# Walking the moving columns and the output of a float32r matmul in runs of 16

## The chip, the cores and the metric

The kernel runs on one core of one Trainium2 chip, as one launch. The metric is the device time of that core in microseconds. The inputs lie in HBM, laid out with channels on partitions, and the output is written back to HBM in the same way.

## The reference

Two layers of a diffusion backbone over 256 latent tokens and 256 context tokens, each of 2048 channels, in float32. Layer 0 mixes tokens by pooling over windows of 2, 4, 8 and 16; layer 1 by neighbourhood attention that also reads the context. Each mixer is followed by a gated feed-forward of inner width 5504 with a width-3 convolution along the tokens. Shift, scale and gate of every sub-layer come from a modulation of two conditioning vectors. What matters here is the feed-forward:

```python
def conv_ffn(u, w_gate, w_up, conv_w, conv_b, w_down):
    T = u.shape[1]
    gp = jnp.pad(u @ w_gate, ((0, 0), (1, 1), (0, 0)))
    gte = gp[:, :T] * conv_w[0] + gp[:, 1:T + 1] * conv_w[1] + gp[:, 2:] * conv_w[2] + conv_b
    return (jax.nn.silu(gte) * (u @ w_up)) @ w_down

    ...
    h = h + ml[:, 5] * conv_ffn(modulate(rms_norm(h, norm2_g[i]), ml[:, 3], ml[:, 4]), ...)
    if not last:
        hc = hc + mc[5] * conv_ffn(modulate(rms_norm(hc, norm2_g[i]), mc[3], mc[4]), ...)
```

In layer 0 it runs for both streams, latent and context; in layer 1, the last, for the latent one alone.

## The kernel before

Activations are kept transposed: a tile has 128 channels on its partitions and tokens along the free dimension. There are 16 such tiles of channels (KT), and the inner width of the feed-forward makes 43 tiles (NF). One PSUM bank is 128 x 512 float32, and every output of the matmuls in question is one bank or half of one.

To keep float32 accuracy on TensorE's faster float32r format, every operand is split into a high part, rounded to float32r, and a low part, the rest. A weight tile is loaded from HBM on SP's queue, ACT casts its high part and DVE (or POOL) subtracts to get the low part (`split`, L145 and L147). A product is then three terms: high times high, high weight times low activation, low weight times high activation.

- **Layer 0, gate and up** (`gu0`, L638 to L640). For each of the 35 tiles from 8 on, one gate and one up bank are filled. The 512 columns are the 256 latent and the 256 context tokens. For each of the 16 channel tiles `A[k]` three matmuls follow one another: high weight with the high columns (L638), high weight with the low columns (L639), low weight with the high columns (L640). The first eight tiles are made earlier, during the mixer (`partial`, L551 to L553).
- **Layer 0, down** (`down0`, L664 to L666). The 43 tiles are taken in chunks of four (three in the last). For each chunk and each of the 16 output tiles, the same three matmuls are made for each tile of the chunk, over `acts`, which are pairs of high and low 512-column tiles.
- **Layer 1, gate and up** (`gu1`, L773 and L776). There are only 256 columns. The high and the low columns of a channel tile lie side by side in `B[k]`, so one matmul of 512 columns (L773) does two of the three terms, each into its half of the bank; a matmul of 256 columns (L776) adds the low weight's term into the second half. Eight of the first kind, eight of the second, then again eight and eight.
- **Layer 1, down** (`down1`, L820 and L824; L816 to L818 for the last chunk) has the same form as gate and up.
- **Attention** lies between the layers: values (L883 to L885), keys (L948 to L950), queries (L967 and L971), output projection (L1092 and L1134).

All of these matmuls write to whole, unbroken pieces of a bank, and read unbroken runs of columns. L967 alone reads its 512 columns as two runs of 256, which lie 512 columns apart in `A[k]`.

The order of the instructions on each engine is set when the program is built, by a scheduler that goes over the whole kernel. Banks are handed out from pools: four for gate and up, three or four for down. During layer 0's feed-forward DVE also computes the modulation of layer 1 (`pump`, L245 and L247), with a small matmul per piece that sums over partition groups (L171). After each down projection ACT scales the bank (L676, L833), and POOL adds it to the residual stream `hl` and `hc` (L677, L835).

Of the kernel before, what the change touches and what calls it, by code (L numbers as in the profile page):

```python
# [17 lines left out]
P = 128  # L18
D = 2048
KT = D // P  # L20
T = 256
# [38 lines left out]
def kernel(ctx: ExitStack, tc: tile.TileContext, xT, cxT, wmod, wg, wu, wd, wp,  # L60
                         wq, wv, wo, vec, cc, rope, inv, strips, out):
    nc = tc.nc
# [8 lines left out]
    def bank(tag, name):  # L71

        if tag == "d" and nbank[0] is not None:
            nbank[0] += 1
            if nbank[0] % 4 == 0:
                tag = "m"
        return pp.tile([P, 512], F32, tag=tag, bufs={"gu": 4, "d": 3, "m": 1}[tag], name=name)

    def flat(a):
        return a.rearrange("p s t -> p (s t)")  # L80


    vt = main.tile([P, NVEC], F32, name="vt")
# [39 lines left out]
    def load(src, cols, name):  # L123

        ts = []
        for j in range(0, cols, 1024):
            n = min(1024, cols - j)
            t = stage(f"{name}_{j}")
            nc.sync.dma_start(t[:, :n], src(j, j + n))
            ts.append((t, n))  # L130
        return ts

    def split(ts, name, share=0):

        parts = []
        for j, (t, n) in enumerate(ts):
            turn[0] += 1
            pools = [whp] * 3 + extra
            pool = pools[turn[0] % len(pools)]
            hi = pool.tile([P, 1024], F32R, tag="wh", name=f"{name}h{j}")  # L140
            lo = pool.tile([P, 1024], F32R, tag="wl", name=f"{name}l{j}")
            with ExitStack() as behind:
                for ins in hold:
                    behind.enter_context(tc.issue_after(ins))
                nc.scalar.copy(hi[:, :n], t[:, :n])  # L145
                eng = nc.gpsimd if share and turn[0] % share == 0 else nc.vector
                eng.tensor_tensor(lo[:, :n], t[:, :n], hi[:, :n].bitcast(F32), op=ALU.subtract)  # L147
            parts.append((hi, lo))
        return parts

    def ld(src, name, share=0):
        return split(load(lambda a, b: src[:, a:b], 2048, name), name, share)
# [114 lines left out]
    def M(l, which, k, s):  # L267
        return modT[l, which * 4 + k // 4][:, k % 4, s : s + 1]
# [60 lines left out]
    with ExitStack() as ph0:  # L329
# [6 lines left out]
        for j in range(1, 4):  # L336
            nc.vector.tensor_copy(quad[:, j], quad[:, 0])
        quad = flat(quad)

        def h_of(s):  # L340
            return hc if s else hl
# [46 lines left out]
        acts = {}  # L388
# [238 lines left out]
        def gu0(f):  # L627
            res = []
            for nm, wsrc in (("g", wg), ("u", wu)):
                parts = ld(wsrc[0, f], f"w{nm}0_{f}")  # L630
                if f > NS + 3:
                    next(pump, None)
                ps = bank("gu", f"{nm}0_{f}")
                for k in range(KT):
                    hi, lo = parts[k // 8]
                    c = P * (k % 8)
                    xh, xl = flat(A[k][:, 0]), flat(A[k][:, 1])
                    nc.tensor.matmul(ps, hi[:, c : c + P], xh, start=(k == 0), stop=False)  # L638
                    nc.tensor.matmul(ps, hi[:, c : c + P], xl, start=False, stop=False)  # L639
                    nc.tensor.matmul(ps, lo[:, c : c + P], xh, start=False, stop=(k == KT - 1))  # L640
                    if k == 7 and f > NS + 3:
                        next(pump, None)
                res.append(ps)
            return res
# [3 lines left out]
        def down0(c, fs, acts, after=None):  # L648
            n = len(fs)
            last = c == len(chunks) - 1  # L650
            for mg in range(4):
                parts = split(load(lambda a, b: wd[0, mg, :, fs[0] + a // 512 : fs[0] + b // 512, :], 512 * n, f"wd0_{c}_{mg}"),
                              f"wd0_{c}_{mg}")
                if c > 1:
                    next(pump, None)
                for m in range(4):
                    if m == 2 and c > 1:
                        next(pump, None)
                    ps = bank("d", f"d0_{c}_{mg}_{m}")
                    for i in range(n):  # L660
                        hi, lo = parts[i // 2]
                        o = 512 * (i % 2) + P * m
                        xh, xl = acts[i]
                        nc.tensor.matmul(ps, hi[:, o : o + P], xh, start=(i == 0), stop=False)  # L664
                        nc.tensor.matmul(ps, hi[:, o : o + P], xl, start=False, stop=False)  # L665
                        nc.tensor.matmul(ps, lo[:, o : o + P], xh, start=False, stop=(i == n - 1))  # L666
                    k = 4 * mg + m
                    if last:
                        for s in both:
                            nc.vector.scalar_tensor_tensor(h_of(s)[:, k, :], ps[:, T * s : T * s + T], M(0, 5, k, s),  # L670
                                                           h_of(s)[:, k, :], op0=ALU.mult, op1=ALU.add)
                        n3.add(h_of, k)
                    else:
                        y = f0.tile([P, 2, T], F32, tag="t2", name=f"dy{c}_{k}")
                        for s in both:
                            nc.scalar.activation(y[:, s], ps[:, T * s : T * s + T], AF.Copy, scale=M(0, 5, k, s))  # L676
                            nc.gpsimd.tensor_tensor(h_of(s)[:, k, :], h_of(s)[:, k, :], y[:, s], op=ALU.add)  # L677
                if after is not None:
                    after()
# [3 lines left out]
        acts[NC], sg = gate0(NC, *r6)  # L683
        normalise(0, 3, h_of, both, rstd, f0, range(14, KT))
        res = gu0(NS)
        rest = [e for e in range(NS) if e not in acts]

# [33 lines left out]
    with ExitStack() as ph2:  # L721
# [11 lines left out]
        B = {}  # L733

        def norm_b(ks):
            for k in ks:
                a = ap0.tile([P, 2, 2, T], F32R, tag=f"A{k}", name=f"B{k}")[:, 0]
                y = f1.tile([P, 512], F32, tag="t2", name=f"nrmB{k}")[:, 0:T]
                nc.vector.scalar_tensor_tensor(y, hl[:, k, :], M(1, 4, k, 0), rstd[:, 0:T], op0=ALU.mult, op1=ALU.mult)
                nc.scalar.activation(a[:, 0], y, AF.Identity, bias=M(1, 3, k, 0))  # L740
                if k % 2:
                    z = f1.tile([P, 512], F32, tag="t2", name=f"nrmBz{k}")[:, 0:T]
                    nc.scalar.activation(z, y, AF.Identity, bias=M(1, 3, k, 0))
                    nc.gpsimd.tensor_tensor(a[:, 1], z, a[:, 0].bitcast(F32), op=ALU.subtract)
                else:
                    ins = nc.vector.scalar_tensor_tensor(a[:, 1], y, M(1, 3, k, 0), a[:, 0].bitcast(F32),
                                                         op0=ALU.add, op1=ALU.subtract)
                B[k] = a
                if k == 9:
                    hold[:] = [ins.ins]  # L750

        def gu1(f):
            res = []
            pre = None
            if f == 0:
                pre = [load(lambda a, b: w[1, f][:, a:b], 2048, f"w{nm}1_{f}") for nm, w in (("g", wg), ("u", wu))]
                for q, ts in enumerate(pre):
                    first = split(ts[:1], f"w{q}1_{f}_0", 4)
                    hold[:] = [tail]
                    pre[q] = first + split(ts[1:], f"w{q}1_{f}_1", 4)  # L760
                    hold.clear()
                norm_b(range(KT))
            elif f == 2:
                hold.clear()
            for q, (nm, wsrc) in enumerate((("g", wg), ("u", wu))):
                parts = pre[q] if pre else ld(wsrc[1, f], f"w{nm}1_{f}", 2 if f % 4 > 1 else 0)
                ps = bank("gu", f"{nm}1_{f}")

                for j in range(2):
                    hi, lo = parts[j]  # L770
                    for k in range(8 * j, 8 * j + 8):
                        c = P * (k % 8)
                        nc.tensor.matmul(ps, hi[:, c : c + P], flat(B[k]), start=(k == 0), stop=False)  # L773
                    for k in range(8 * j, 8 * j + 8):
                        c = P * (k % 8)
                        nc.tensor.matmul(ps[:, T:], lo[:, c : c + P], B[k][:, 0], start=False, stop=(k == KT - 1))  # L776
                res.append(ps)
            return res

# [60 lines left out]
        for c, fs in enumerate(chunks):  # L840
            acts = []
# [16 lines left out]
        for j, (a, b) in enumerate(((0, 4), (4, 6), (6, 8), (8, 12), (12, 16))):  # L858
            v = hl[:, a:b, :]
# [379 lines left out]
```

## Time and profile before

| | us |
|---|---|
| median of 2 runs (3069.73 to 3072.13) | 3070.93 |
| the profiled execution | 3070.34 |
| its span, from the first to the last instruction | 3068.5 |
| PE busy in the span | 3007.0 |
| DVE busy | 1939.4 |
| ACT busy | 1372.9 |
| POOL busy | 826.4 |

PE is the engine that runs the matmuls, PEld its weight loads; every matmul of the trace has a weight load of its own. DVE, ACT and POOL are the vector, scalar and general engines, SP the queue from which the loads are issued. A matmul's record goes from its start to its end, and the next one begins before it ends; so the records overlap, and the rate of the stream is read from the distance of the starts. Rows of one line give the instruction count after an x, then the shortest, the median and the longest duration in ns, and the first and the last start in us. Rows of the chain of waits give the start, the length and what ran, merged where one line follows itself. PEclk is the TensorE clock that was granted.

### The profile page before, as it was taken

What the parts mean: (1) busy time and instruction counts of PE and PEld (TensorE: products, weight loads), DVE (VectorE), ACT (ScalarE), POOL (GpSimd) and SP (SyncE); (2) the same over time, 40 slices, a digit from 0 to 9 for tenths busy, and PEclk for the clock granted to TensorE, in tenths of its full rate; (3) what the DMA queues carried; (4) which work ended last, traced back from release to release, by engine and by line L of the source; (5) the groups of instructions that cost most, each with busy time, mean ns of one, the idle gap of its engine ahead of it and who ended that gap; (6) DMA issues with size and microseconds to landing.
All of it is one profiled execution on the core that took longest, in us unless ns stands there. A gap on an engine that the chain in (4) does not pass through costs nothing.

```text
span 3068.5 us, 40828 instructions
## 1 busy us (share of the span) xinstructions
PE 3007.0 (98%) x15082; PEld 2414.2 (79%) x15082; DVE 1939.4 (63%) x2748; ACT 1372.9 (45%) x2219; POOL 826.4 (27%) x823
## 2 busy tenths in 40 slices
PE   6999999999999999999999999999999999999998
PEld 2565658888888888888887888878888888888887
DVE  4445774285674857658485666474767666666666
ACT  3333454423333242433334444343545666666665
POOL 2011213303022130311302000000002566566665
PEclk9999999999999999999999999999999999999999
DMA  9878663284755747466482333333355556565553
GB/s 382 334 271 305 215 233 103 90 253 141 223 178 180 226 148 250 148 203 202 161 253 83 113 108 104 106 112 106 106 159 184 183 180 201 189 188 180 185 192 117
DMA packets 177927, 559.70 MB, mean 182 GB/s; under 512 B 17600, under 2 KB 22208, under 8 KB 177728
## 3 DMA queue, kind: packets, MB, share of 16 engines
q1 hardware_dynamic: 177728, 557.10, 55.6%
q8 instruction: 119, 1.95, 0.3%
q14 instruction: 80, 0.66, 0.1%
HBM read 554.93 MB, written 2.10 MB: 182 GB/s over the span
## 4 chain that ended last, share of the span: by engine, by line
PE 94%; DVE 2%; POOL 1%; DMA 1%; ACT 1%; issue 1%; SPq 0%; DVEq 0%; ACTq 0%; POOLq 0%
PE g L773 5%; PE u L773 5%; PE d L664 5%; PE d L666 5%; PE d L665 5%; PE d L820 4%; PE g L638 4%; PE g L640 4%; PE g L639 4%; PE u L639 4%; PE u L638 4%; PE u L640 4%; PE mod L199 3%; PE u L776 3%; PE g L776 3%; PE d L824 2%
## 5 line engine op out<-in xcount | busy, mean ns | idle before, releaser
L677 POOL TENSOR_TENSOR hl<-hl,dy 128x256 f32<-128x256 f32 x160 | 146.7, 917 | 943.3 <-ACT dy L676 943.1
L835 POOL TENSOR_TENSOR hl<-hl,dy 128x256 f32<-128x256 f32 x320 | 332.2, 1074 | 188.2 <-ACT dy L833 186.0
L247 DVE SCALAR_TENSOR_TENSOR macc<-wm,sc,macc 128x512 f32<-128x512 f32 (+1 forms) x360 | 328.9, 946 | 70.8 <-DMA wm<-wmod 69.8
L676 ACT ACTIVATE dy<-d,modT 128x256 f32<-128x256 f32 x320 | 133.1, 469 | 187.1 <-PE d L666 172.4
L199 PE MATMUL mod<-wm,sc 128*32 128x512 f32 x768 | 131.1, 617 | 23.3 <-DMA wm<-wmod 23.3
L677 POOL TENSOR_TENSOR hc<-hc,dy 128x256 f32<-128x256 f32 x160 | 129.0, 806 | 0.0
L833 ACT ACTIVATE dy<-d,modT 128x512 f32<-128x512 f32 x160 | 104.5, 684 | 43.0 <-PE d L824 41.5
L147 DVE TENSOR_TENSOR wd_2l<-wd,wd_2h 128x1024 fp32r<-128x1024 f32 (+1 forms) x44 | 54.6, 1247 | 108.8 <-ACT wd_2h L145 107.6
L922 POOL TENSOR_TENSOR rk<-rk,rp 128x256 f32<-128x256 f32 x16 | 13.2, 826 | 365.5 <-DVE rk L921 309.7
L147 DVE TENSOR_TENSOR wd_3l<-wd,wd_3h 128x1024 fp32r<-128x1024 f32 (+1 forms) x44 | 52.0, 1203 | 76.8 <-ACT wd_3h L145 75.5
L147 DVE TENSOR_TENSOR wd_1l<-wd,wd_1h 128x1024 fp32r<-128x1024 f32 (+1 forms) x44 | 53.7, 1225 | 56.4 <-ACT wd_1h L145 56.4
L472 POOL TENSOR_TENSOR pf<-ws,inv 128x256 f32<-128x256 f32 x32 | 27.7, 885 | 220.6 <-PE mod L199 105.0
L199 PEld LDWEIGHTS mod<-wm,sc 128*32 128x32 f32 x768 | 23.7, 110 | 77.4 <-issue 61.5
L145 ACT CAST wd_1h<-wd 128x1024 fp32r<-128x1024 f32 (+1 forms) x44 | 45.3, 1031 | 78.3 <-PE u L639 53.5
L147 DVE TENSOR_TENSOR wd_0l<-wd,wd_0h 128x1024 fp32r<-128x1024 f32 (+1 forms) x44 | 54.7, 1249 | 36.9 <-ACT wd_0h L145 36.9
L1011 ACT ACTIVATE sb<-sb,nm 128x512 f32<-128x512 f32 x64 | 46.1, 722 | 64.3 <-DVE nm L1007 63.1
L799 DVE TENSOR_TENSOR actb<-sgb,actb 128x256 fp32r<-128x256 f32 x43 | 52.8, 1228 | 26.2 <-ACT actb L798 26.2
L145 ACT CAST wd_0h<-wd 128x1024 fp32r<-128x1024 f32 (+1 forms) x44 | 45.2, 1031 | 53.6 <-PE u L773 29.1
L664 PE MATMUL d<-act,wd_2h 128*128 128x512 f32 x172 | 67.2, 391 | 0.0
L666 PE MATMUL d<-act,wd_2l 128*128 128x512 f32 x172 | 67.0, 390 | 0.0
L665 PE MATMUL d<-act,wd_2h 128*128 128x512 f32 x172 | 67.0, 390 | 0.0
L666 PE MATMUL d<-act,wd_3l 128*128 128x512 f32 x172 | 67.0, 390 | 0.0
(1752 smaller groups left out, 9278.0 us busy)
## 6 DMA issues: line engine op xcount, KB each, us to landing
wm<-wmod SPq DMA_DIRECT2D x384, 512.0 KB, 6.1
wd<-wd SPq DMA_DIRECT2D x168, 512.0 KB, 4.4
wg<-wg SPq DMA_DIRECT2D x156, 512.0 KB, 4.7
wu<-wu SPq DMA_DIRECT2D x156, 512.0 KB, 4.5
wv<-wv SPq DMA_DIRECT2D x32, 512.0 KB, 4.0
wk<-wq SPq DMA_DIRECT2D x32, 512.0 KB, 4.1
wq<-wq SPq DMA_DIRECT2D x32, 512.0 KB, 3.6
wo<-wo SPq DMA_DIRECT2D x32, 512.0 KB, 3.9
```

The lines of the kernel that those rows point to most:

```text
L147: eng.tensor_tensor(lo[:, :n], t[:, :n], hi[:, :n].bitcast(F32), op=ALU.subtract)
L199: nc.tensor.matmul(ps[32 * j : 32 * j + 32, :], sc[:, 4 * g + j, :], ts[j // 2][0][:, 512 * (j % 2) : 512 * (j % 2) + 512], start=(g == 0) ...
L247: nc.vector.scalar_tensor_tensor(acc[s], v, sc2[:, k, s : s + 1], acc[s], op0=ALU.mult, op1=ALU.add)
L638: nc.tensor.matmul(ps, hi[:, c : c + P], xh, start=(k == 0), stop=False)
L639: nc.tensor.matmul(ps, hi[:, c : c + P], xl, start=False, stop=False)
L640: nc.tensor.matmul(ps, lo[:, c : c + P], xh, start=False, stop=(k == KT - 1))
L664: nc.tensor.matmul(ps, hi[:, o : o + P], xh, start=(i == 0), stop=False)
L665: nc.tensor.matmul(ps, hi[:, o : o + P], xl, start=False, stop=False)
L666: nc.tensor.matmul(ps, lo[:, o : o + P], xh, start=False, stop=(i == n - 1))
L677: nc.gpsimd.tensor_tensor(h_of(s)[:, k, :], h_of(s)[:, k, :], y[:, s], op=ALU.add)
L773: nc.tensor.matmul(ps, hi[:, c : c + P], flat(B[k]), start=(k == 0), stop=False)
L835: nc.gpsimd.tensor_tensor(hl[:, k, :], hl[:, k, :], y[:, q], op=ALU.add)
```

## The change

A helper gives another view of the same columns: the free dimension is seen as a x n x 16, and walked with the n in front. For n = 4 and 512 columns, the walk takes columns 0 to 15, then 64 to 79, 128 to 143 and so on to 463, then it starts again at 16, at 32 and at 48. For n = 2 the runs of 16 lie 32 columns apart and there are two rounds. The moving operand and the output of a matmul are walked in the same order, so each column's product lands where it did before.

It is used in the three places named above: layer 0's gate (n = 4) and up (n = 2), layer 0's down (n = 4), and layer 1's gate and up (n = 4, both the 512- and the 256-column matmuls). Layer 1's down, attention, the mixer and the first eight tiles of layer 0 are as before.

```diff
+    def turns(v, n=4):
+
+        return v.rearrange("p (a b e) -> p b a e", b=n, e=16)
...
                     xh, xl = flat(A[k][:, 0]), flat(A[k][:, 1])
-                    nc.tensor.matmul(ps, hi[:, c : c + P], xh, start=(k == 0), stop=False)
-                    nc.tensor.matmul(ps, hi[:, c : c + P], xl, start=False, stop=False)
-                    nc.tensor.matmul(ps, lo[:, c : c + P], xh, start=False, stop=(k == KT - 1))
+                    n = 4 if nm == "g" else 2
+                    xh, xl, po = turns(xh, n), turns(xl, n), turns(ps, n)
+                    nc.tensor.matmul(po, hi[:, c : c + P], xh, start=(k == 0), stop=False)
+                    nc.tensor.matmul(po, hi[:, c : c + P], xl, start=False, stop=False)
+                    nc.tensor.matmul(po, lo[:, c : c + P], xh, start=False, stop=(k == KT - 1))
...
-                        xh, xl = acts[i]
-                        nc.tensor.matmul(ps, hi[:, o : o + P], xh, start=(i == 0), stop=False)
-                        nc.tensor.matmul(ps, hi[:, o : o + P], xl, start=False, stop=False)
-                        nc.tensor.matmul(ps, lo[:, o : o + P], xh, start=False, stop=(i == n - 1))
+                        xh, xl = map(turns, acts[i])
+                        po = turns(ps)
+                        nc.tensor.matmul(po, hi[:, o : o + P], xh, start=(i == 0), stop=False)
+                        nc.tensor.matmul(po, hi[:, o : o + P], xl, start=False, stop=False)
+                        nc.tensor.matmul(po, lo[:, o : o + P], xh, start=False, stop=(i == n - 1))
...
-                        nc.tensor.matmul(ps, hi[:, c : c + P], flat(B[k]), start=(k == 0), stop=False)
+                        nc.tensor.matmul(turns(ps), hi[:, c : c + P], turns(flat(B[k])), start=(k == 0), stop=False)
...
-                        nc.tensor.matmul(ps[:, T:], lo[:, c : c + P], B[k][:, 0], start=False, stop=(k == KT - 1))
+                        nc.tensor.matmul(turns(ps[:, T:]), lo[:, c : c + P], turns(B[k][:, 0]), start=False, stop=(k == KT - 1))
```

## The prediction

> **What bounds the kernel now.** I read the head of the page first, then the busy time in stretches of the span, then the rows of the changed lines and the chain of waits for the spacing of the matmuls.
>
> ```profile
> span 3068.5 us, 40828 instructions
> PE 3007.0 (98%) x15082; PEld 2414.2 (79%) x15082; DVE 1939.4 (63%) x2748; ACT 1372.9 (45%) x2219; POOL 826.4 (27%) x823
> PEclk9999999999999999999999999999999999999999
> PE 94%; DVE 2%; POOL 1%; DMA 1%; ACT 1%; issue 1%; SPq 0%; DVEq 0%; ACTq 0%; POOLq 0%
> ```
>
> PE is busy for 98% of the span, and 94% of the chain that ended last is PE. Its clock is not held back. The stretches say the same for the two places that the change touches:
>
> ```profile
> core 0: us, PE busy (x) PEld busy (x) DVE busy (x) ACT busy (x) POOL busy (x), PEclk, DMA share, GB/s
> 500.00:1650.00 1150.00, 1150.00 (x5095) 953.33 (x5094) 732.01 (x902) 407.49 (x619) 246.59 (x296) 1.00 0.59 183
> 2330.00:3020.00 690.00, 690.00 (x3937) 606.05 (x3936) 465.71 (x475) 424.33 (x623) 416.11 (x341) 1.00 0.58 187
> ```
>
> The first stretch is the feed-forward of layer 0 (gate, up, down), the second that of layer 1. In both, PE has no idle time, and the next busiest engine, DVE, has 64% (732 of 1150) and 67% (466 of 690). So every nanosecond by which a matmul's place in the stream grows or shrinks goes into the end of the kernel whole.
>
> A busy PE is not its rate, since the records overlap (a matmul is in flight for some 390 ns while the next has begun). The rate is the distance from start to start:
>
> ```profile
> L638 PE MATMUL g<-A,wg_10h x16: 389/390/390, 525.8 to 536.0; 128*128 128x512 f32 x16
> 2363.88 0.23 PE u L773
> 2364.11 0.95 PE u L776 x8
> 2365.06 1.84 PE g L773 x8
> 2366.90 0.95 PE g L776 x8
> L816 PE MATMUL d<-actb,wd_0h x12: 283/284/284, 3036.3 to 3040.3; 128*128 128x256 f32 x12
> ...
> L816 PE MATMUL d<-actb,wd_2h x12: 283/283/284, 3044.9 to 3048.9; 128*128 128x256 f32 x12
> ```
>
> The first row is one gate tile of layer 0: L638, L639 and L640 take turns, so from the first to the last of 16 lie 45 matmuls in 10.2 us, 226.7 ns each, for 512 columns. The next rows are pieces of the chain (start, length, what): in layer 1 eight 512-column matmuls take 1.84 us (230 ns each) and eight 256-column ones 0.95 us (119 ns). The two L816 rows stand 72 matmuls of 256 columns apart (two groups of 4 x 3 x 3): 8.6 us, 119.4 ns each. So one column costs (226.7 - 119.4) / 256 = 0.419 ns, 512 columns 214.5 ns, and some 12 ns of every matmul do not depend on the columns.
>
> **The change, part by part.** Only access patterns change. Each engine's instructions stand in the order of before, SP's and POOL's DMA and work included, with the same tiles and counts; nothing is moved past a queue, nothing is added to ACT, DVE or POOL. What PSUM holds at the end of a group is at the same addresses, so its readers see no difference. Nineteen matmuls of the down projection lose a wait of PE on PE: it is an in-order engine that idles 0 in that stretch, so I cost this at nothing.
>
> How many matmuls are walked otherwise:
>
> ```profile
> 0.00:3069.00 3069.00, 437.08 (x1120) 210.41 (x1120) 0.99 0.56 182
> 0.00:3069.00 3069.00, 268.13 (x688) 129.22 (x688) 0.99 0.56 182
> 0.00:3069.00 3069.00, 349.43 (x1376) 249.70 (x1376) 0.99 0.56 182
> 0.00:3069.00 3069.00, 192.25 (x1376) 187.29 (x1376) 0.99 0.56 182
> ```
>
> These are the rows of L638, L664, L773 and L776 alone over the whole span (counts in brackets). L638 to L640 are 3 x 1120 = 3360, half with a step of 64 (gate) and half with 32 (up); L664 to L666 are 3 x 688 = 2064; L773 is 1376: together 6800 of 512 columns. L776 is 1376 of 256. A walk of 512 columns in runs of 16 has 32 runs and 31 jumps, whichever step; one of 256 has 15. Sum: 6800 x 31 + 1376 x 15 = 231,440 jumps, each made by the reading side (SBUF) and by the writing side (PSUM) at once. All lie on PE, without cover.
>
> What a jump costs is not in the trace for the writing side: every output of before is one unbroken run. For the reading side there is one near row. L967 (attention's queries) reads 512 columns as two runs of 256 that lie 512 apart, and writes one run:
>
> ```profile
> 1890.32 1.81 PE q L967 x8
> ```
>
> That is 226 ns each, no more than the unbroken L638, with half a step of the last digit, 0.6 ns, as the room for one jump. So a jump in reading is free or costs at most about 0.6 ns. The far end is to treat each run of 16 as a matmul of its own; the nearest row is the sum of the layer-1 modulation:
>
> ```profile
> 1007.37 0.13 PE modt_12s L171 x2
> 1007.82 0.13 PE modt_13s L171 x2
> ```
>
> 0.13 us for two of 16 columns, 65 ns each, 32 of them 2.1 us in place of 0.227: some 12.7 ms in all. Nothing in the program splits the instruction, so I use it for no case but as the end that is excluded.
>
> The other end is a gain. It can be no more than what stands beside the columns: 5424 x (226.7 - 214.5) = 66 us, 1376 x (230 - 214.5) = 21 us, 1376 x (119 - 107.3) = 16 us, 103 us together, if the walk removed all of it. Those 12 ns are the same at 512 and at 256 columns, which speaks for a price of the instruction or its weight load, and not for one of the walk.
>
> For a jump I take one column's time, 0.419 ns: it is the smallest step by which a stream of one column after the other can slip, it lies within the 0.6 ns that L967 leaves, and the writing side must add to what stands in PSUM at full rate, column after column, with no slack that any row shows. Sum: 231,440 x 0.419 ns = 97 us. On the profiled execution's own 3070.3 us that is 3167 us; the median of the runs shown, 3070.9, is 0.6 us above it, which changes nothing. Per line I expect 240 ns in place of 226.7 for the 512-column matmuls of layer 0, 243 for 230 at L773, and 125 for 119 at L776.
>
> [...]
>
> **What else could lie behind it.** The end of the kernel is not PE's:
>
> ```profile
> 3021.76 27.24 POOL hl L835 x28
> ```
>
> The last adds of layer 1 on POOL follow the down projection, which is not changed in layer 1. If PE is slower in gate and up, POOL comes to this stretch with the same work or less behind it; I add nothing.
>
> **Rivals.** (1) A jump is free on both sides: 3070 us. For it: the L967 row, the same engine, type and column count. Against it: one jump is not 31, and the row has none in the output. [...]
>
> (2) Faster. What stands beside the columns is not quite fixed: L773 is spaced 230 ns where L638 has 226.7 for the same columns, type and tile size, and the weight loads behind them differ too:
>
> ```profile
> L664 PEld LDWEIGHTS d<-act,wd_0h x172: 187/188/188, 460.3 to 1648.3; 128*128 128x128 f32 x172
> L816 PEld LDWEIGHTS d<-actb,wd_0h x12: 192/192/193, 3036.2 to 3040.1; 128*128 128x128 f32 x12
> ```
>
> 187 ns in the even stream, 192 in the stream of short matmuls. That looks like two reads, of the weights and of the moving columns, that hinder each other by their phase. If the excess comes from addresses that fall together, a walk in steps of 128 or 256 bytes can take them apart. The price is up to 103 us, so down to 2967 us; it decides (2% is 61 us) once 60% of the excess goes. Against it: A, B and the activations lie in different tiles and columns, and all 512-column rows of layer 0 still have the same 226.7 ns.
>
> (3) A jump costs more: two columns' time, for example where reading and writing both slip, 194 us, 3264 us; at three, 3361 us. A price that is some half of a run's own time (8 columns, 3.4 ns) would give 3070 + 776 = 3846 us. For it speaks only that nothing bounds the writing side.
>
> (4) The step matters, not the jump: with 32 free and 64 at one column's time, the 1680 up matmuls drop out, 1680 x 31 x 0.419 ns = 22 us, and the time is 3145 us. I count it with the forecast, since it is on the same side.
>
> **How the numbers follow.** A slower kernel through jumps has 0.52: 0.28 at about one column's time (with the fourth rival), 0.10 at about two, 0.14 at more. No change has 0.23, faster by the second rival 0.25, spread from 2967 to 3009 us. The forecast is the likeliest price of the likeliest side, 3167 us, its own range 3135 to 3200. The range for 8 in 10 reaches over both signs: from 2975 (which leaves out 0.05 of the gain) to 3270 (two columns' time; it leaves out 0.14). Slower by over 2%, which is about what a measurement of this kernel can tell from no change, is over 3132 us, faster is under 3010 us: 0.52 slower, 0.23 within, 0.25 faster.
>
> **What would show it.** In the profile after, the start-to-start distance of the changed lines is the whole test: some 240 ns in a layer-0 gate tile (45 matmuls in 10.8 us in place of 10.2), eight L773 in 1.94 us and eight of the 256-column line in 1.0 us, with the unchanged L820 spaced as before, and the stretches outside the two feed-forwards equally long. Gate and up of layer 0 side by side tell whether the step counts. The first rival shows as 226.7 ns, the second as less than that with a shorter weight load, the third as well over 240. The prediction is wrong if these distances stay while the time moves, or if an unchanged line's distance changes.

## The result and the profile after

The changed kernel takes 3146.78 us (median of 2 runs, 3145.79 to 3147.78) against 3070.93 us; the ratio is 1.0247, 95% interval 1.0203 to 1.0291. That is 76 us more, where 97 us were forecast. The profiled execution took 3145.79 us, with a span of 3144.0.

The head of the page and, in the second fence, the busy time of the two feed-forward stretches (the second one moved to later times):

```profile
span 3144.0 us, 40828 instructions
PE 3085.2 (98%) x15082; PEld 2419.9 (77%) x15082; DVE 1934.7 (62%) x2748; ACT 1373.4 (44%) x2219; POOL 825.1 (26%) x823
```

```profile
core 0: us, PE busy (x) PEld busy (x) DVE busy (x) ACT busy (x) POOL busy (x), PEclk, DMA share, GB/s
500.00:1650.00 1150.00, 1150.00 (x4826) 909.39 (x4825) 704.01 (x873) 380.30 (x568) 218.97 (x265) 1.00 0.57 175
2400.00:3100.00 700.00, 700.00 (x3957) 606.45 (x3956) 464.75 (x476) 426.95 (x627) 419.31 (x343) 1.00 0.58 185
```

The same instructions, the same clock (PEclk 1.00), no idle time (PE busy 1150.00 of 1150.00 us), but in the same 1150 us PE gets through 4826 matmuls instead of 5095. Nothing waits more; each matmul takes longer. The rows of one gate and one up tile of layer 0 (step 64 and step 32), and pieces of the chain of waits from layer 1 (start, length, what):

```profile
L645 PE MATMUL g<-A,wg_10h x16: 395/402/411, 531.4 to 542.1; 128*128 128x512 f32 x16
L645 PE MATMUL u<-A,wu_10h x16: 398/403/407, 542.9 to 553.6; 128*128 128x512 f32 x16
```

```profile
2490.28 0.92 PE d L827 x4
...
2521.22 1.90 PE u L780 x8
2523.13 0.94 PE u L783 x8
2524.07 1.89 PE g L780 x8
```

From the first to the last of the 16 lie 45 matmuls: 10.7 us, 238 ns each, in both tiles. In layer 1, L780 (before the change L773) takes 1.90 us for eight where it took 1.84, and L783 (L776) 0.94 where it took 0.95. L827 (L820), which is not changed, stays at 0.92 for four; before it was 0.93.

A row's times end at a tenth of a us, which leaves such a distance open by 2 ns. For the sum and for the experiments I therefore average the distance from each matmul's start to the next one's over all records of the line in the trace (1680 gate, 1680 up, 2064 down, 1376 long and 1376 short ones of layer 1), without the few distances over 1.25 times the median:

| mean distance, ns | before | after | difference | over all records, us |
|---|---|---|---|---|
| layer 0 gate (runs of 16, step 64) | 227.0 | 239.2 | +12.2 | +20.5 |
| layer 0 up (runs of 16, step 32) | 226.7 | 240.0 | +13.3 | +22.3 |
| layer 0 down (step 64) | 226.7 | 239.5 | +12.8 | +26.1 |
| layer 1 gate and up, 512 columns | 230.3 | 237.8 | +7.5 | +9.2 |
| layer 1 gate and up, 256 columns | 119.1 | 117.8 | -1.3 | -1.8 |

The last column sums every distance, the long ones too: 76.3 us, which is the whole of the 76.

Layer 1's long matmuls also lose less because they had lost something before. By place in their group of eight, the distances of before are 233, 236, 228, 232, 231 and three times 227 ns (medians): behind the short matmuls it takes five long ones to reach the pace of layer 0. That is why their mean was 230.3 and not 226.7. After the change the eight are 237, 232, 236, 239, 242, 240, 238 and 241 ns.

### The profile page after: what moved, and what is told of

Same layout as the page of the kernel before. It is cut to its first block, busy times and chain, and to the rows that moved or that the text cites. A ratio compares the mean times of both kernels' runs of the same rounds, so it can differ in the third digit from the quotient of the medians.

```text
span 3144.0 us, 40828 instructions
## 1 busy us (share of the span) xinstructions
PE 3085.2 (98%) x15082; PEld 2419.9 (77%) x15082; DVE 1934.7 (62%) x2748; ACT 1373.4 (44%) x2219; POOL 825.1 (26%) x823
## 4 chain that ended last, share of the span: by engine, by line
PE 95%; DVE 1%; POOL 1%; DMA 1%; ACT 1%; issue 1%; SPq 0%; DVEq 0%; ACTq 0%; POOLq 0%
PE g L780 5%; PE d L671 5%; PE d L673 5%; PE d L672 5%; PE u L780 5%; PE d L827 4%; PE g L644 4%; PE g L646 4%; PE g L645 4%; PE u L646 4%; PE u L645 4%; PE u L644 4%; PE mod L203 3%; PE g L783 3%; PE u L783 3%; PE d L831 2%
## 5 line engine op out<-in xcount | busy, mean ns | idle before, releaser
L671 PE MATMUL d<-act,wd_2h 128*128 128x512 f32 x172 | 69.4, 403 | 0.0
L671 PE MATMUL d<-act,wd_3h 128*128 128x512 f32 x172 | 69.3, 403 | 0.0
L672 PE MATMUL d<-act,wd_1h 128*128 128x512 f32 x172 | 69.3, 403 | 0.0
L671 PE MATMUL d<-act,wd_0h 128*128 128x512 f32 x172 | 69.2, 403 | 0.0
```

The costliest lines, as they stand in the source:

```text
L671: nc.tensor.matmul(po, hi[:, o : o + P], xh, start=(i == 0), stop=False)
L672: nc.tensor.matmul(po, hi[:, o : o + P], xl, start=False, stop=False)
```

## The experiments

These are the theories, by the letters that the expectations use. A, the forecast's: each jump costs one column's time, on the writing side (PSUM). B: the same price, on the reading side (SBUF). C: a walked pattern has a fixed price, whatever its jumps. After the first four runs: D, the columns lose time where they are read at the same time as the next weights, by the way in which both are read; E, the loss belongs to the moving stream alone. D divides into D1, where the weights lie counts, and D2, only the order of each read counts. A time is that of one run, for the last two the median of five; the kernel before took 3069.8 to 3071.5 us on the same chips.

**One side at a time.** Only the moving operand is walked (and the output is straight), then only the output:

```diff
-                    xh, xl, po = turns(xh, n), turns(xl, n), turns(ps, n)
+                    xh, xl, po = turns(xh, n), turns(xl, n), ps      # moving side alone
+                    po = turns(ps, n)                                # output alone
```

and the same in down and in layer 1.

> The moving operand is walked as in the changed kernel, the output is written straight through; so the columns land in another order, and the output is not the reference's. Theory A (a jump costs one column's time on the writing side): layer 0's matmuls are back at 226.7 ns from start to start, the total near 3071 us. Theory B (the reading side pays): 240 ns and 239 ns in layer 1 as in the changed kernel, total near 3147 us. Theory C (a walked pattern costs some fixed 13 ns through its meeting with the weight load, which reads the same memory): as B.

> The output is walked, the moving operand is read straight through; the columns land in another order, and the output is not the reference's. Theory A (writing side): 240 ns in layer 0, total near 3147 us. Theories B and C (reading side): 226.7 ns and near 3071 us. If both this run and the one with the moving side alone are slow, the two sides' jumps fall together in the changed kernel and hide each other.

Measured: 3145.3 us with the moving side alone, 3073.0 with the output alone. The row of the gate tile in the one and in the other:

```profile
L645 PE MATMUL g<-A,wg_10h x16: 395/402/411, 529.0 to 539.7; 128*128 128x512 f32 x16
```

```profile
L645 PE MATMUL g<-A,wg_10h x16: 389/389/389, 527.6 to 537.8; 128*128 128x512 f32 x16
```

The first is the changed kernel's row (10.7 us, the same three durations), the second that of before (10.2 us). Over all records the reading side alone gives 239.2, 240.0, 239.5, 237.8 and 117.8 ns, line by line what the change gave; the output alone gives 227.0, 226.7, 226.7, 230.3 and 119.1. Theory A falls: with runs of 16, jumps in the output alone (PSUM) left each line's mean distance where it was, and jumps in reading alone (SBUF) made the whole loss of the change. The walks that follow move both sides again; that their losses too are made in reading is inferred from these two runs.

**Other lengths of run.** The helper got a second argument e for the length of a run:

```diff
-        return v.rearrange("p (a b e) -> p b a e", b=n, e=16)
+        return v.rearrange("p (a b e) -> p b a e", b=n, e=e)
```

> Both sides walked, in longer runs: layer 0 gate in runs of 32 with a step of 128, up in runs of 32 with a step of 64 (15 jumps each), down in runs of 64 (7 jumps), layer 1's 512-column matmuls in runs of 128 (3 jumps), its 256-column ones straight. Theories A and B (0.419 ns for each jump): gate and up 226.7 + 6.3 = 233.0 ns, down 229.6 ns, layer 1's long ones 1.3 ns over before; total 3071 + 21 + 6 + 2 = 3100 us. Theory C (a fixed price of a walked pattern): all of layer 0 stays at 240 ns, total near 3150 us.

> Both sides walked, in shorter runs: layer 0 gate in runs of 8 (63 jumps), up in runs of 4 (127), down in runs of 2 (255), layer 1's 512-column matmuls straight, its 256-column ones in runs of 8 (31). Theories A and B: gate 226.7 + 26.4 = 253 ns, up 280 ns, down 334 ns; total 3071 + 44 + 89 + 221 = 3425 us and something for the short ones. Theory C: 240 ns everywhere in layer 0, total near 3141 us. The 256-column matmuls: if some 12 ns of every matmul are fixed, 119 + 13 = 132 ns; if they are paced by their weight loads and their columns alone would take some 113 ns (the least that the trace of before shows), 113 + 13 = 126 ns.

Measured: 3094.4 us, near the 3100 of a sum by jumps, and 3549.2 us, 124 above its 3425. Neither comes about by jumps. With long runs, a row of gate and of up, then one of down (16 of L671 with 45 matmuls from first to last):

```profile
L645 PE MATMUL g<-A,wg_10h x16: 395/395/395, 526.0 to 536.5; 128*128 128x512 f32 x16
L645 PE MATMUL u<-A,wu_10h x16: 397/399/399, 537.2 to 547.8; 128*128 128x512 f32 x16
...
L671 PE MATMUL d<-act,wd_1h x16: 389/389/389, 984.7 to 994.9; 128*128 128x512 f32 x16
```

Runs of 32 cost 6.4 ns with a step of 128 (233.4 over all records) and 9.8 ns with a step of 64 (236.5), for the same 15 jumps. Runs of 64 (7 jumps, 226.9) and of 128 (230.2 in layer 1) cost nothing. With short runs, up (runs of 4), down (runs of 2; from the first to the last of 8 of L671 lie 21 matmuls), and a piece of layer 1's chain; gate (runs of 8) is shown below:

```profile
L645 PE MATMUL u<-A,wu_10h x16: 379/385/390, 581.9 to 591.9; 128*128 128x512 f32 x16
```

```profile
L671 PE MATMUL d<-act,wd_1h x8: 641/642/642, 1000.1 to 1009.8; 128*128 128x512 f32 x8
```

```profile
2945.66 0.91 PE u L783 x8
```

Gate has 228.4 ns over all records where 253 were expected, up 225.7 where 280 were, which is 1 ns below before, with 127 jumps. (One row can lie some ns off such a mean, for the reason given below.) The 256-column matmuls in runs of 8 fall from 119.1 to 113.7 ns. Down in runs of 2 has 461 ns, twice before, and carries the total. Theory B falls too: no one price of a jump fits 6.4 and 9.8 ns for 15 jumps and -1.0 for 127. C falls with the runs that cost nothing (226.9 and 230.2 ns).

Gate's mean hides two paces. Two of its tiles in the run with short runs:

```profile
L645 PE MATMUL g<-A,wg_21h x16: 389/391/400, 1078.0 to 1088.4; 128*128 128x512 f32 x16
L645 PE MATMUL g<-A,wg_22h x16: 380/382/388, 1100.2 to 1110.1; 128*128 128x512 f32 x16
```

Tiles 8, 18, 22, 26 and so on to 42 have some 221.4 ns, the other 27 some 230.5, with the same walk of the same columns. Within a tile the distances repeat: 220, 220, 220 in tile 22, and a round of numbers from 227 to 237 in tile 21. In the changed kernel's up tiles 237 and 243 ns alternate in the same way, in some 236 and 244. So run and step alone do not fix the pace. What else differs between these tiles (where their weights lie, which bank they fill, at which moment they start) no run took apart.

**Is it the weight load?** In the trace of before (layer 0's gate), a weight load of 188 ns starts 3 to 4 ns after the matmul ahead of its own, so one matmul's columns stream while the next one's weights are loaded. Here the columns stay straight and the weights are read otherwise, first with a step, then in one run that starts elsewhere (in the last of each eight channel tiles, and the last of each four output tiles of down, that much earlier in place of later):

```diff
-                    c = P * (k % 8)
-                    nc.tensor.matmul(ps, hi[:, c : c + P], xh, ...)
+                    c = k % 8                                       # with a step (down: 4)
+                    w = slice(2 * P * (c // 2) + c % 2, 2 * P * (c // 2) + 2 * P, 2) if nm == "g" else slice(c, 8 * P, 8)
+                    nc.tensor.matmul(ps, hi[:, w], xh, ...)
...
+                    c += (16 if nm == "g" else 32) * (1 if k % 8 < 7 else -1)    # starts elsewhere
```

> Moving operand and output straight, as before; the weight load instead takes its 128 columns with a step: 2 in layer 0's gate, 8 in up, 4 in down. The weights so taken are the wrong ones, and the output is not the reference's. Theory D (the moving columns lose time where the weight load reads the same memory at the same time): the spacing leaves 226.7 ns in at least one of the three, by some ns either way, and the total moves by 15 to 80 us. Theory E (the loss belongs to the moving stream's own order of reading): 226.7 ns in all three, the total within 5 us of before, as long as the weight load itself stays shorter than a matmul.

> Everything straight as before, but the weight load's 128 columns start elsewhere: 16 columns (64 bytes) on in layer 0's gate, 32 (128 bytes) in up, 4 (16 bytes) in down. The weights so taken are the wrong ones, and the output is not the reference's. If the loss between the two reads goes by where the two addresses stand to one another (theory D1), one of the three spacings leaves 226.7 ns by over 1 ns. If it goes by the order of each read alone, since the two shift against each other in time anyway (theory D2), all three stay at 226.7 ns and the total within 3 us of before.

Measured: 3129.6 us and 3094.9 us. The load and the matmul of a gate tile with a step of 2, then those with a start 16 columns on:

```profile
L639 PEld LDWEIGHTS g<-A,wg_10h x16: 193/193/212, 529.9 to 540.4; 128*128 128x128 f32 x16
L639 PE MATMUL g<-A,wg_10h x16: 392/394/394, 530.2 to 540.6; 128*128 128x512 f32 x16
```

```profile
L640 PEld LDWEIGHTS g<-A,wg_10h x16: 187/188/189, 527.6 to 538.1; 128*128 128x128 f32 x16
L640 PE MATMUL g<-A,wg_10h x16: 388/394/398, 527.9 to 538.3; 128*128 128x512 f32 x16
```

With steps of 2, 8 and 4 the distances are 233.6, 244.3 and 235.0 ns. The loads with 8 and 4 are themselves long (some 327 and 310 ns), so the clean case is the step of 2, with a load of 193 and a matmul 6.6 ns later than before. The second run is cleaner still: the load keeps its 187 to 189 ns, no read has a jump, and yet the distances are 233.0 (16 columns on, 64 bytes), 232.8 (32) and 228.0 (4). So in these two runs the matmul's pace went with how the weights are read (227.0 to 233.6 ns with a step of 2) and from where (227.0 to 233.0 with a start 64 bytes on), and E falls. Of D's two forms D1 stands, for straight columns. That the walked columns lose their 12 to 13 ns in the same way is inferred: no run moved the weights under a walk. Whether the address counts against the moving columns' addresses or against the memory's own borders, these runs do not separate.

**Fixed or by column?** The gate's 512 columns are cut into 384 and 128, up's into 320 and 192 (the first of the 16 channel tiles stays whole):

```diff
+                w = 384 if nm == "g" else 320
+                for a, b, k in [(0, 512, 0)] + [(0, w, k) for k in range(1, KT)] + [(w, 512, k) for k in range(1, KT)]:
...
+                    nc.tensor.matmul(ps[:, a:b], hi[:, c : c + P], xh, start=(k == 0), stop=False)
```

> All walked straight. In layer 0's gate each group of 48 matmuls becomes 3 of 512 columns, 45 of 384 and 45 of 128; in up 3 of 512, 45 of 320 and 45 of 192. The result is the same. If 12 to 13 ns of each matmul are fixed (Theory D: one loss for each weight load): 173 ns for 384 columns and 147 for 320. If the loss goes with the columns (Theory E; 226.7/512 = 0.443 ns for each): 170 and 142 ns. The narrow ones: 119 ns for both widths if the weight loads pace them, else 66 and 93 ns.

Rows of L640 in stretches that hold one width each:

```profile
L640 PE MATMUL g<-A,wg_10h x15: 334/334/346, 537.2 to 544.5; 128*128 128x384 f32 x15
...
L640 PE MATMUL g<-A,wg_10h x13: 272/276/277, 545.2 to 549.2; 128*128 128x128 f32 x13
...
L640 PE MATMUL u<-A,wu_10h x14: 309/309/312, 550.7 to 556.4; 128*128 128x320 f32 x14
...
L640 PE MATMUL u<-A,wu_10h x14: 272/273/278, 557.2 to 561.6; 128*128 128x192 f32 x14
```

3 x 14 matmuls of 384 columns in 7.3 us are 174 ns each, 39 of 320 in 5.7 us are 146; in the trace nearly all distances are 173 or 174, and 146 or 147. With 226.7 at 512 that is 0.417 ns for a column and 13.3 ns for each matmul, as D has it and E has not. The narrow ones come at 36 in 4.0 us and 39 in 4.4 us, 111 and 113 ns whether 128 or 192 columns wide: there the columns do not set the pace. That the weight loads do is the reading that is left, not one that a run singles out; the 119 that I expected was too high. The total is 3216.3 us.

**Does the step matter?** Runs of 4 and 8 with other steps:

> Both sides walked: layer 0's gate in runs of 4 with a step of 8, up in runs of 4 with a step of 32, down in runs of 8 with a step of 16; layer 1's 512-column matmuls in runs of 4 with a step of 16, its 256-column ones in runs of 8 with a step of 32, the form that stood at 114 ns in the run with short runs. Theory D: the step matters, so gate, up and the 226 ns of runs of 4 with a step of 16 differ by over 2 ns. Theory E (only the length of a run counts): 226 ns in gate and up, 229.6 in down. Either way the 256-column matmuls stay at 114 ns and layer 1 gains some 10 us.

> Both sides walked: layer 0's gate in runs of 4 with a step of 64, up in runs of 4 with a step of 128, down in runs of 8 with a step of 64; layer 1's 512-column matmuls in runs of 8 with a step of 32, its 256-column ones in runs of 4 with a step of 16. Theory D: spacings between 214 and 240 ns that go with the step. Theory E: 226 ns in gate and up, 229.6 in down and in layer 1's long ones, whichever step.

Measured: 3110.3 and 3261.7 us. The gate rows, step 8 and step 64:

```profile
L645 PE MATMUL g<-A,wg_10h x16: 393/396/398, 529.3 to 539.8; 128*128 128x512 f32 x16
```

```profile
L645 PE MATMUL g<-A,wg_10h x16: 433/444/451, 537.8 to 550.3; 128*128 128x512 f32 x16
```

Layer 0's 512-column matmuls over all records, in ns, by run and step in columns (straight: 226.7):

| run \ step | 8 | 16 | 32 | 64 | 128 |
|---|---|---|---|---|---|
| 2 | 461.3 | | | | |
| 4 | 232.4 | 225.7 | 246.3 | 277.1 | 267.8 |
| 8 | | 232.4 | 228.4 | 248.9 | |
| 16 | | | 240.0 | 239.2 | |
| 32 | | | | 236.5 | 233.4 |
| 64 | | | | | 226.9 |

Along a row the number of jumps is the same. The step decides in runs of 4 by 51 ns, and hardly counts in runs of 16, the only ones that the change has, between the two steps that it has. E, which gave runs of 4 the same 226 ns at every step, falls here too; D's own bounds of 214 to 240 ns were far too narrow. The 228.4 is the mean of the two paces above, and 225.7 came out as 226.1 for gate and up in a later run.

**The parts of layer 1.** Layer 0 is straight; in layer 1 only gate's long and only up's short matmuls are walked as in the change.

```diff
+                        if nm == "g":
+                            nc.tensor.matmul(turns(ps), hi[:, c : c + P], turns(flat(B[k])), ...)
...
+                        if nm == "u":
+                            nc.tensor.matmul(turns(ps[:, T:]), lo[:, c : c + P], turns(B[k][:, 0]), ...)
```

> Layer 0 as before. In layer 1 the walk of the changed kernel (runs of 16, step 64) for gate's 512-column matmuls alone and for up's 256-column ones alone. If the two forms act on each other only through the matmuls right behind them: gate 238 ns for the long ones and 119 for the short ones, up 230 and 118. If the long ones' slowness in layer 1 comes from the short ones before them: in up the long ones change with the short ones' walk, by 1 ns or more. Total 3071 + 688 x 7.5 ns - 688 x 1.3 ns = some 3075 us.

Measured: 3075.3 us. Gate has 237.7 and 119.1 ns, up 230.2 and 119.7. The long ones' loss is their own, whatever the short ones do. The short ones gained nothing alone (119.7, not the 118 expected); the 1.3 ns of the changed kernel come only when both are walked. Why is not settled.

**A version that beats both.** The best patterns of the table, in layer 0's three places and in layer 1's gate, up and down; then the same with layer 0 straight.

```diff
-                        nc.tensor.matmul(ps, hi[:, c : c + P], flat(B[k]), start=(k == 0), stop=False)
+                        nc.tensor.matmul(turns(ps, 4, 4), hi[:, c : c + P], turns(flat(B[k]), 4, 4), start=(k == 0), stop=False)
-                        nc.tensor.matmul(ps[:, T:], lo[:, c : c + P], B[k][:, 0], start=False, stop=(k == KT - 1))
+                        nc.tensor.matmul(turns(ps[:, T:], 4, 8), lo[:, c : c + P], turns(B[k][:, 0], 4, 8), start=False, stop=(k == KT - 1))
```

> The version that the earlier runs point to: 512-column matmuls of layer 0's gate, up and down and of layer 1's gate, up and down in runs of 4 with a step of 16, layer 1's 256-column ones in runs of 8 with a step of 32. From the spacings of the runs before: layer 0 5424 x -1.0 ns = -5 us, layer 1's gate and up 1376 x (-4.2 - 4.2) ns = -12 us, down 640 x (-6 - 4) ns = -6 us; together 3071 - 23 = 3048 us. If the loss comes back elsewhere, no less than 3069 us.

> The same with layer 0 straight as before: 3071 - 18 = 3053 us if the gains of the two layers add up, and its layer-0 spacings at 226.7 ns.

Measured: 3049.9 us (3049.5 to 3051.6), ratio to before 0.9933, interval 0.9919 to 0.9946; and 3053.6 us, ratio 0.9944, interval 0.9932 to 0.9957, against 3070.5 us (9 runs). Pieces of the chain in layer 1 of the first:

```profile
2440.53 0.47 PE d L824 x4
2441.00 0.93 PE d L820 x4
```

```profile
2429.98 1.80 PE g L780 x8
2431.78 0.91 PE d L827 x4
...
2437.28 0.91 PE g L783 x8
```

The first fence is the kernel before, for down: 0.93 us for four long ones, 0.90 to 0.91 now; gate's eight fall from 1.84 to 1.80 and from 0.95 to 0.91. Layer 1 brings 17 of the 21 us, layer 0 some 4, as the spacings had it (18 and 5). The gain is 0.7%, small but real: both intervals end below 1. The new form of walk is the same as the change's; only the numbers differ.

## Why the prediction was right, and where it was not

- **What bounds the kernel.** Right: the distances of the changed lines add up to 76.3 us, and the time moved by 76. No wait, no other engine and not the end on POOL (27.25 us of the chain after, 27.24 before) took part.
- **Nothing moves.** Right: the number of instructions is the same, the 15082 matmuls start in the same order of tiles, and the lines that are not changed keep their distances (L827 231.9 ns against 232.0).
- **The sum.** Layer 0's terms hold: 70 us forecast (5424 x 31 x 0.419 ns), 69 measured. Layer 1's do not: 18 us for the long ones, 9 measured; 9 for the short ones, -2 measured. That is the 21 us between the forecast and the result.
- **The mechanism.** Wrong, although its size fits. The step that failed is "one column's time for a jump, because the writing side must add to PSUM at full rate". The output alone cost nothing (226.7 ns, 3073.0 us), and the moving side alone cost all of it (3145.3 us). With both walked, 127 jumps cost less than none, 15 jumps cost 6.4 or 9.8 ns, 7 cost nothing. For runs of 16 the loss came near 31 x 0.419 ns by chance: two figures of the same size are no proof of a mechanism. The forecast's size was luck. In a kernel with other runs the same rule would have been off by 54 ns a matmul (up in runs of 4).
- **"Some 12 ns of every matmul do not depend on the columns."** Right, and better known now: 13.3 ns at 320, 384 and 512 columns. That these belong to the instruction or its weight load was a guess of the text. The run with shifted weights shows that the load's place can add to them (64 bytes add 6.0 ns to a matmul whose columns are read as before); where the 13.3 ns themselves come from is not shown.
- **The second rival** (faster) comes nearest to what the runs point to, two reads that hinder each other by their addresses (6.0 ns for weights that start 64 bytes on), with the sign wrong for this walk (12 to 13 ns more in layer 0). Of its arguments for, the 230 ns of L773 come from the five matmuls behind the short ones, as the distances by place show; the argument against, that all tiles of layer 0 give the same 226.7, was weak, because in the kernel all their weights start at a multiple of 128 columns. It should have had a larger chance as a mechanism, with the sign open.
- **The first rival** (free) is right for writing (226.7 to 227.0 ns in layer 0 with the output alone) and out for reading (239.2 to 240.0 with the moving side alone), in runs of 16. The row that spoke for it, L967, has runs of 256, and the long runs show why it could not tell: the runs of 64 (226.9 ns) and of 128 (230.2, in layer 1) that were tried lose nothing.
- **The third rival** (two columns' time or more) is out: no line of the change lost more than 13.3 ns, where one column's time for 31 jumps is 13.0.
- **The fourth rival** (the step) is wrong for runs of 16 (239.2 and 240.0), although its 3145 us lie nearest to the result; this too is luck. In runs of 4, 8 and 32 the step does count, but not as the rival has it.

Open: why some runs and steps lose time and others do not; why layer 1's long matmuls end at 237.8 ns and layer 0's at 239.5 with the same walk (the other 3.6 of the 5.3 ns between their losses stand in the kernel before); what gives tiles of one walk two paces; why runs of 2 double the time, and on which side, since both were walked there.

## What to carry to other kernels

In a stream of matmuls that is bound by PE, the distance from start to start is worth reading to the nanosecond: what is left beside the columns (here 13.3 of 226.7 ns) was not a constant, and moved with the way in which the moving columns are read (239.2 to 240.0 ns in runs of 16) and with the place of the weights (233.0 ns with a start 64 bytes on). A walk must be tried by run and step together, since neither told the price alone (runs of 4: 225.7 to 277.1 ns by step; a step of 64: 236.5 to 277.1 by run); in runs of 16 only the moving side counted. A mean over tiles should be looked at tile by tile, since one walk had two paces (221.4 and 230.5 ns). When a sum comes out right, take the mechanism apart before using it again: here one run with each side alone was enough to overturn it.

## What the runs showed of the hardware

- A float32r matmul of 320, 384 or 512 columns was followed by the next after 146, 174 and 226.7 ns, which is 0.417 ns for each column and 13.3 ns; one of 128 or 192 columns after 111 or 113 ns. In the kernel before, each float32 matmul of 512 columns (L199, weights of 32 columns) starts 428 ns or more behind the fourth one before it.
- An output walked in runs of 16, with steps of 32 and 64, cost layer 0 nothing (226.7 to 227.0 ns, 3073.0 us); the moving columns walked so cost 12 to 13 ns a matmul there (239.2 to 240.0 ns, 3145.3 us).
- Weights that start 64 bytes on, with a load as long as before (187 to 189 ns), slowed the matmuls from 227.0 to 233.0 ns; 16 bytes on, from 226.7 to 228.0.
- Runs of 4 columns with a step of 16 were a little faster than straight (225.7 and 226.1 against 226.7 ns), and with a step of 64 much slower (277.1).
- Weights taken with a step of 8 or 4 columns have loads of some 327 and 310 ns instead of 188.
- A stream of equal matmuls settled at more than one pace: 221.4 or 230.5 ns by tile, in runs of 8 with a step of 32. In layer 1 before, behind eight matmuls of 256 columns, those of 512 are followed by the next after 233, 236, 228, 232 and 231 ns and then 227.
